# One core, a nine-stage network in fp32 split into two fp32r parts: named PSUM banks for each stage, a later place for one silu and for a stream of modulation columns, and the token sums of the sparse feed-forward layers all on VectorE

## The chip, the cores and the metric

The kernel runs on one core of one Trainium2 chip. The metric is the device time of one execution, in microseconds (us). TensorE is PE in the views, VectorE DVE, ScalarE ACT, GpSimd POOL, and SyncE, which here only issues DMAs, SP.

## The reference

The input is x (512 tokens x 1024 channels) and one conditioning vector c. Nine stages follow each other, each adding to x:

```python
cond = silu(c)
for l in (0, 1):
    sh1, sc1, g1, sh2, sc2, g2 = split(cond @ ada_w[l] + ada_b[l], 6)
    h = rmsnorm(x, norm_mix[l]) * (1 + sc1) + sh1
    y = even_mixer(h) if l == 0 else odd_mixer(h)      # attention: mix0, mix1
    x = x + g1 * (y @ w_out[l])
    h = rmsnorm(x, norm_ffn[l]) * (1 + sc2) + sh2
    x = x + g2 * ((silu(h @ gate[l]) * (h @ up[l])) @ down[l])   # ffn0, ffn1
x = x + mamba2(rmsnorm(x))      # ssm: chunked scan, 4 groups, 4 chunks of 128 tokens
x = x + swiglu(rmsnorm(x))      # ffn2
x = x + conformer(rmsnorm(x))   # conv
x = x + swiglu(rmsnorm(x))      # ffn3
out = rmsnorm(x)                # final
```

Mixer 0 has a differential attention and one over the 128 keys that an index score selects, mixer 1 a banded attention with sinks. All is fp32.

## The kernel before

x lies transposed in SBUF as eight tiles `xT` of 128 channels x 512 tokens. Every fp32 operand of a product is split into `hi` (a cast to fp32r, on ACT, L297 for weights) and `lo` (the rest, by a subtraction on DVE, L298 for weights), and each product is three matmuls, `hi` with `hi`, `lo` with `hi`, `hi` with `lo` (`mm3`, L305 to L307). Weights come in 512 KB pieces, `raw`, by DMAs that SP issues in one order; three `raw` and four `hi`/`lo` buffers circulate, so SP waits for a `lo` to be made before it can issue the next `raw`.

The stages run in the order mix0 (to about 350 us), ffn0 (367 to 740), mix1, ffn1 (947 to 1305), ssm (to 1715), ffn2 (1716 to 2080), conv, ffn3 (2302 to 2655), final. Between two stages the norm of the next one is spread over the last products of the one before: `sq` and its sum, PE's column sum `ss`, a chain of thirteen small DVE steps for the inverse root (L345 to L362), `rb`, four transposes by which PE spreads the result over partitions, then either `z` (L483) with `hi` and `lo` (L489 to L497, by ACT, POOL and DVE) in two column halves (class `Split`, before ffn0, mix1, ffn1, conv), or a copy `R` (L427) that multiplies the products afterwards (class `Norm`, before ssm, ffn2, ffn3).

In a feed-forward stage `gu([j])` computes gate `pg` and up `pu` of hidden block j, DVE and ACT make `s = silu(pg) * pu` and its split `d`, and `dn` multiplies five or so blocks by the down weights. Where `FIRST_S` says so (ffn1 from block 3, ffn2 and ffn3 from block 2), `gu7` replaces a gate/up pair by seven products of half the columns (`seven`): it needs sums of weight pieces (`ws`, L716 to L720) and sums of token pieces, which `crossed` makes once in a stage for four k: two subtractions (L693, L694), two more steps on DVE (L695, L696), a cast `xh` on ACT (L698) and the rest `xl` (L699). The subtractions are on POOL; `xl` is on DVE for even k and on POOL for odd k. `sums(ks)` is called within the items of the first blocks: in ffn1 all four k in the first item, in ffn2 and ffn3 two k in each of the first two.

In ffn0 a second stream runs beside the blocks: `md0.stream` and `md1.stream` make 56 columns of the modulation, for each a DMA `araw` (six buffers) and a reduction on DVE against `cb`, the broadcast silu of c (L657). `cond()` (L629) issues the DMA of `cb` and its Silu on ACT (L632). `behind` holds the stream back until the instruction `nm.mark`, the last `z` of the norm, has been placed, and `_weave` mixes the two streams by their weights, 345 and 28.

In ssm, `ssd(g)` handles a group in four chunks: products `pS`, `po`, `py` on PE, the sums `yo` and `yg` on DVE, the gated `zs` (L1507), its square on ACT (L1508), at the end of the group the thirteen small steps, the scaling of `zs` (L1523) and the transposes `yT`, which the last items `so(3)` need. The items `so(q)` (products `pj` of 512 columns) of earlier groups are woven in.

The program is written as such generators; the order in which an engine then executes its instructions is set when the kernel is built, by the scheduler of the Tile framework (`schedule_with_timeline_sim=True`), which goes by data, buffers and its own account of time. So an edit in one stage can change the order in others. PSUM has eight banks of 128 x 512 fp32; a stage's pool gives each tag (`mm`, `lg`, `tr`, `py`, `st`) a number of them that circulate:

```python
"ffn": ({"d": 12, "z": 6, "su": 2, "sq": 2, ...}, {"mm": 6, "st": 1, "tr": 1}),
...
return p.tile(shape, dt, tag=tag, name=name, bufs=bufs[tag])
```

Of the kernel before, what the change touches and what calls it, by code (L numbers as in the profile page):

```python
# [10 lines left out]
F32 = mybir.dt.float32  # L11
F32R = mybir.dt.float32r
I32 = mybir.dt.int32
AF = mybir.ActivationFunctionType
# [76 lines left out]
def _layout(i):  # L91
# [20 lines left out]
    for n in range(4):  # L112
# [36 lines left out]
PHASES = {  # L149
# [9 lines left out]
    "ssm": (SSB,  # L159
# [3 lines left out]
}  # L163
# [49 lines left out]
def chain(*gs):  # L213
    for g in gs:
        yield from g
# [7 lines left out]
def _program(nc, tc, a, out, stages=STAGES):  # L223
# [6 lines left out]
    sm = pool("sm", 4)  # L230
    cur = {"sb": None, "ps": None}

    def phase(name, kinds=("sb", "ps")):
        for k in kinds:
            if cur[k]:
                cur[k][0].close()
            e = ExitStack()
            kw = {"space": PSUM} if k == "ps" else {}
            p = e.enter_context(tc.tile_pool(name=f"{k}_{name}", bufs=1, reuse_waits="tile", **kw))
            cur[k] = (e, p, PHASES[name][k == "ps"])  # L240

    def ptile(k, shape, dt, name):
        tag = ALIAS.get(name, name)
        _, p, bufs = cur[k]
        if k == "ps" and tag not in bufs:
            tag = {"tr": "pt", "st": "tr", "py": "tr"}[tag]
        return p.tile(shape, dt, tag=tag, name=name, bufs=bufs[tag])

# [182 lines left out]
    class Split:  # L431
# [44 lines left out]
        def build(self, hf):  # L476
            o = HALVES[hf]
            for c in range(KC):
# [8 lines left out]
                if c % 2:  # L487
                    if sh is not None:
                        S.activation(z, z, AF.Identity, bias=sh)  # L489
                    S.copy(hi_, z)  # L490
                    self.gmark = G.tensor_tensor(lo, z, hi_.bitcast(F32), op=OP.subtract)
                elif sh is not None:
                    S.activation(hi_, z, AF.Identity, bias=sh)
                    V.scalar_tensor_tensor(lo, z, sh, hi_.bitcast(F32), op0=OP.add, op1=OP.subtract)  # L494
                else:
                    S.copy(hi_, z)
                    V.tensor_tensor(lo, z, hi_.bitcast(F32), op=OP.subtract)  # L497

# [130 lines left out]
    def cond():  # L629
        cbx[0] = wide("cb")  # L630
        nc.sync.dma_start(cbx[0], a["c"].to_broadcast([128, 1024]))
        S.activation(cbx[0], cbx[0], AF.Silu)  # L632

# [52 lines left out]

    def crossed(k, z1, z2, pool_lo):


        hv = T // 2  # L690
        t = wide1("ws")
        q = [t[:, i * hv:(i + 1) * hv] for i in range(4)]
        G.tensor_tensor(q[0], z1[:, :hv], z1[:, hv:], op=OP.subtract)  # L693
        G.tensor_tensor(q[2], z2[:, hv:], z1[:, hv:], op=OP.subtract)  # L694
        V.scalar_tensor_tensor(q[1], z2[:, hv:], -1.0, q[0], op0=OP.mult, op1=OP.subtract)  # L695
        V.scalar_tensor_tensor(q[3], q[1], -1.0, z2[:, :hv], op0=OP.mult, op1=OP.subtract)  # L696
        hi, lo = wide1("xh", F32R), wide1("xl", F32R)
        S.copy(hi, t)  # L698
        (G if pool_lo else V).tensor_tensor(lo, t, hi.bitcast(F32), op=OP.subtract)  # L699
        return [(hi[:, i * hv:(i + 1) * hv], lo[:, i * hv:(i + 1) * hv]) for i in range(4)]  # L700
# [49 lines left out]
    def ffn(n, nm, gcol, nxt):  # L750
# [6 lines left out]
        def sums(ks):  # L757
            for k in ks:
                z = []
                for c in (k, k + 4):  # L760
# [4 lines left out]
                    else:  # L765
                        z.append(tmp("z"))
                        S.activation(z[-1], X[c], AF.Copy, scale=nm.gcol(c))
                x4.append(crossed(k, *z, k % 2))
        d = {}

        def gu(js):
            def it():
# [14 lines left out]
                if sparse and len(x4) < 4:  # L787
                    sums(range(4) if direct else range(2 * js[0], 2 * js[0] + 2))
                if nm.R is None:
# [188 lines left out]
    def mix0(make, following):  # L978
        phase("mix0", ("sb",))
        phase("start", ("ps",))  # L980
        cond()
        consts()
# [817 lines left out]
    if stages[0] != "mix0":  # L1800
# [3 lines left out]
        if stages[0] in STAGES[:4]:  # L1804
            cond()
            mods()
            _run(chain(md0.stream(range(24)), md1.stream(range(24))))
        nm = norms[stages[0]]().all()
    for i, name in enumerate(stages):
# [14 lines left out]
        else:  # L1824
            n = int(name[3])
            f = ffn(n, nm, (None, md0.col(40), md1.col(40))[n + 1] if n < 2 else None, nx)
            if n == 0:
                cond()
                _weave((f, 345), (behind(lambda: nm.mark, chain(md0.stream(range(20, 24)), md1.stream(range(24)))), 28))
            else:  # L1830
                _run(f)
# [20 lines left out]
```

## Time and profile before

| | |
|---|---|
| three runs | 2678.31 us median (2671.75 to 2680.00) |
| profiled execution | 2678.19 us, of which the span in the trace is 2676.4 us |
| PE busy | 2526.0 us, 94% of the span |
| DVE, ACT, POOL busy | 1964.1 us (73%), 1264.7 us (47%), 529.5 us (20%) |
| mean granted TensorE clock | 0.977 of full speed |

The span begins with the first instruction and ends with the last; 1.8 us of the execution lie outside it. A line of a timeline gives the start from the span's beginning; in brackets stand the idle time of the engine just before and what released it, where that was a wait. The granted clock is 1.00 at 2.4 GHz and 0.5 at 1.2 GHz; a figure between is a mean over a stretch.

### The profile page before, as it was taken

What the parts mean: (1) busy time and instruction counts of PE and PEld (TensorE: products, weight loads), DVE (VectorE), ACT (ScalarE), POOL (GpSimd) and SP (SyncE); (2) the same over time, 40 slices, a digit from 0 to 9 for tenths busy, and PEclk for the clock granted to TensorE, in tenths of its full rate; (3) what the DMA queues carried; (4) which work ended last, traced back from release to release, by engine and by line L of the source; (5) the groups of instructions that cost most, each with busy time, mean ns of one, the idle gap of its engine ahead of it and who ended that gap; (6) DMA issues with size and microseconds to landing.
All of it is one profiled execution on the core that took longest, in us unless ns stands there. A gap on an engine that the chain in (4) does not pass through costs nothing.

```text
span 2676.4 us, 40109 instructions
## 1 busy us (share of the span) xinstructions
PE 2526.0 (94%) x15299; PEld 2230.7 (83%) x15299; DVE 1964.1 (73%) x3490; ACT 1264.7 (47%) x2353; POOL 529.5 (20%) x411
## 2 busy tenths in 40 slices
PE   5788989999999989999999999999999998899997
PEld 3666878888888989999788888789998888799997
DVE  7898765555556686677678886677877897677777
ACT  4456642222257554444455444444444555544443
POOL 3344220000022250000100000211101782311102
PEclk9988999999999999999999999999999998999999
DMA  7611125554521123333322121232333210233332
GB/s 269 230 56 40 32 87 204 173 173 163 176 82 40 40 64 95 110 93 103 106 75 73 51 83 60 79 92 86 108 98 115 72 63 17 71 103 103 103 103 80
DMA packets 89058, 265.81 MB, mean 99 GB/s; under 512 B 9760, under 2 KB 16032, under 8 KB 88864
## 3 DMA queue, kind: packets, MB, share of 16 engines
q1 hardware_dynamic: 88864, 263.24, 30.6%
q8 instruction: 120, 1.97, 0.3%
q14 instruction: 74, 0.61, 0.1%
HBM read 261.10 MB, written 2.10 MB: 98 GB/s over the span
## 4 chain that ended last, share of the span: by engine, by line
PE 55%; issue 17%; DVE 16%; DMA 4%; ACT 4%; POOL 3%; DVEq 0%; SPq 0%; POOLq 0%; ACTq 0%
PE pj L305 8%; PE pj L306 7%; PE pj L307 7%; PE pg L307 4%; PE pg L305 4%; PE pg L306 4%; DVE lo L298 4%; PE pu L307 3%; PE pu L306 3%; PE pu L305 3%; DMA raw<-w_gu 2%; DMA araw<-ada 1%; POOL yp L1615 1%; PE pj L1418 1%; PE pj L1419 1%
## 5 line engine op out<-in xcount | busy, mean ns | idle before, releaser
L297 ACT CAST hi<-raw 128x1024 fp32r<-128x1024 f32 (+5 forms) x454 | 395.1, 879 | 671.3 <-PE pj L306 236.6
L298 DVE TENSOR_TENSOR lo<-raw,hi 128x1024 fp32r<-128x1024 f32 (+4 forms) x444 | 465.7, 1052 | 181.8 <-ACT hi L297 179.4
L305 PE MATMUL pj<-d,hi 128*128 128x512 f32 (+1 forms) x968 | 354.4, 377 | 4.6 <-DVE s L822 1.6
L306 PE MATMUL pj<-d,hi 128*128 128x512 f32 (+1 forms) x968 | 357.2, 372 | 0.4 <-DVE d L390 0.4
L307 PE MATMUL pj<-d,lo 128*128 128x512 f32 (+1 forms) x968 | 353.6, 372 | 0.0
L747 POOL TENSOR_TENSOR bu<-bu 128x256 f32<-128x256 f32 x59 | 88.6, 1503 | 818.2 <-ACT bu L743 747.3
L305 PE MATMUL pu<-hi 128*128 128x256 f32 (+1 forms) x736 | 229.3, 313 | 2.3 <-DVE z L483 2.3
L307 PE MATMUL pu<-hi,lo 128*128 128x256 f32 (+1 forms) x736 | 230.4, 313 | 1.0 <-DVE lo L298 0.6
L306 PE MATMUL pu<-lo,hi 128*128 128x256 f32 (+1 forms) x736 | 228.8, 312 | 0.0
L305 PEld LDWEIGHTS pj<-d,hi 128*128 128x128 f32 x968 | 182.0, 190 | 37.8 <-DVE s L822 2.0
L305 PE MATMUL pj<-hi 128*128 128x512 f32 (+2 forms) x520 | 206.5, 400 | 4.4 <-ACT qk L907 1.2
L306 PEld LDWEIGHTS pj<-d,hi 128*128 128x128 f32 x968 | 183.8, 190 | 32.0 <-issue 1.0
L307 PEld LDWEIGHTS pj<-d,lo 128*128 128x128 f32 x968 | 183.4, 190 | 31.4 <-issue 0.5
L306 PE MATMUL pj<-lo,hi 128*128 128x512 f32 (+2 forms) x520 | 206.3, 397 | 3.3 <-DVE lo L494 1.4
L307 PE MATMUL pj<-hi,lo 128*128 128x512 f32 (+2 forms) x520 | 204.0, 393 | 0.3 <-DVE lo L298 0.3
L305 PE MATMUL pg<-xh,hi 128*128 128x256 f32 x708 | 199.7, 282 | 0.4 <-ACT ua L740 0.2
L307 PE MATMUL pg<-hi,lo 128*128 128x256 f32 (+1 forms) x572 | 191.9, 335 | 8.6 <-DVE lo L298 8.5
L307 PE MATMUL pg<-xh,lo 128*128 128x256 f32 x708 | 198.1, 280 | 0.0
L306 PE MATMUL pg<-xl,hi 128*128 128x256 f32 x708 | 198.1, 280 | 0.0
L305 PE MATMUL pg<-hi 128*128 128x256 f32 (+1 forms) x572 | 191.4, 335 | 6.7 <-DVE z L483 3.4
L306 PE MATMUL pg<-lo,hi 128*128 128x256 f32 (+1 forms) x572 | 191.0, 334 | 1.0 <-DVE lo L494 0.9
L297 ACT CAST hi<-ws 128x1024 fp32r<-128x1024 f32 x118 | 123.0, 1049 | 111.8 <-DVE ws L717 57.4
(485 smaller groups left out, 6419.7 us busy)
## 6 DMA issues: line engine op xcount, KB each, us to landing
raw<-w_gu SPq DMA_DIRECT2D x176, 512.0 KB, 3.8
araw<-ada SPq DMA_DIRECT2D x96, 512.0 KB, 6.0
raw<-w_dn SPq DMA_DIRECT2D x72, 320.0 KB, 2.9
raw<-w_p SPq DMA_DIRECT2D x24, 512.0 KB, 3.6
raw<-w_dn SPq DMA_DIRECT2D x24, 384.0 KB, 3.3
raw<-w_out SPq DMA_DIRECT2D x32, 256.0 KB, 2.8
raw<-w_xs SPq DMA_DIRECT2D x16, 512.0 KB, 3.5
raw<-w_z SPq DMA_DIRECT2D x16, 512.0 KB, 3.4
```

What stands on the lines that cost most here:

```text
L297: S.copy(hi, raw)
L298: (eng or V).tensor_tensor(lo, raw, hi.bitcast(F32), op=OP.subtract)
L305: E.matmul(ps, lh, rh, start=start, stop=False, **k)
L306: E.matmul(ps, lh, rl, start=False, stop=False, **k)
L307: E.matmul(ps, ll, rh, start=False, stop=stop, **k)
L747: G.tensor_tensor(bu[:, :hv], bu[:, :hv], bu[:, hv:], op=OP.add)
L1418: E.matmul(o, xh[:, ts], wh[:, k], start=st_, stop=False, skip_group_check=True)
L1419: E.matmul(o, xh[:, ts], wl[:, k], start=False, stop=False, skip_group_check=True)
L1615: G.tensor_tensor(yp[:, sft:], yp[:, sft:], pr[:, sft:], op=OP.add)
```

## The change

Each stage now names the banks of each tag as a tuple, the tags go round them in order (`turn`), and a stage's pool allocates all eight banks at its start. The number of banks of a tag does not change in any stage. `sq` gets three buffers in place of two in mix0, ffn0, ffn2 and ffn3, `d` ten in place of twelve in ffn2 and ffn3. In ffn0 the Silu of `cb` is issued by a small generator after four steps of the second stream, the stream waits for the last `lo` on DVE (`lmark`) and not for the last `z`, and its weight is 30. `crossed` makes all its subtractions and all `xl` on DVE. In ffn1 the token sums are made two k at a time, in the first two items.

```diff
 PHASES = {
-    "start": ({}, {"pi": 5, "pw": 1, "st": 1, "tr": 1}),
+    "start": ({}, {"pi": (0, 1, 2, 3, 4), "pw": (5,), "st": (6,), "tr": (7,)}),
-    "mix0": ({..., "yn": 3, "sq": 2, "re": 2, "rl": 2}, {"mm": 2, "lg": 3, "tr": 2, "py": 1}),
+    "mix0": ({..., "yn": 3, "sq": 3, "re": 2, "rl": 2}, {"mm": (0, 1), "lg": (2, 3, 4), "tr": (6, 7), "py": (5,)}),
-             {"mm": 2, "lg": 2, "tr": 2, "py": 1, "st": 1}),
+             {"mm": (5, 3), "lg": (0, 4), "tr": (1, 2), "py": (7,), "st": (6,)}),
-    "ffn0": ({"araw": 6, "cb": 2, "d": 16, "z": 3, "su": 2, "sq": 2}, {"mm": 6, "st": 1, "tr": 1}),
+    "ffn0": ({"araw": 6, "cb": 2, "d": 16, "z": 3, "su": 2, "sq": 3}, {"mm": (5, 3, 0, 4, 1, 2), "st": (6,), "tr": (7,)}),
+             {"mm": (7, 1, 5, 0, 3, 4), "st": (6,), "tr": (2,)}),
-    "ffn": ({"d": 12, "z": 6, "su": 2, "sq": 2, ...}, {"mm": 6, "st": 1, "tr": 1}),
+    "ffn": ({"d": 10, "z": 6, "su": 2, "sq": 3, ...}, {"mm": (2, 1, 5, 0, 3, 4), "st": (6,), "tr": (7,)}),
-            {"mm": 2, "lg": 2, "tr": 2, "py": 1, "st": 1}),
+            {"mm": (3, 4), "lg": (5, 0), "tr": (2, 1), "py": (7,), "st": (6,)}),
-             {"mm": 4, "pt": 2, "ac": 1, "st": 1}),
+             {"mm": (5, 0, 3, 4), "pt": (2, 1), "ac": (7,), "st": (6,)}),
...
+            if k == "ps":
+                turn.clear()
+                for b in range(8):
+                    p.tile([128, T], F32, tag=f"b{b}", name=f"b{b}", bufs=1)
...
+        if k == "ps":
+            i = turn[tag] = turn.get(tag, -1) + 1
+            return p.tile(shape, dt, tag=f"b{bufs[tag][i % len(bufs[tag])]}", name=name, bufs=1)
         return p.tile(shape, dt, tag=tag, name=name, bufs=bufs[tag])
...
-                    V.scalar_tensor_tensor(lo, z, sh, hi_.bitcast(F32), op0=OP.add, op1=OP.subtract)
+                    self.lmark = V.scalar_tensor_tensor(lo, z, sh, hi_.bitcast(F32), op0=OP.add, op1=OP.subtract)
...
     def cond():
...
-        S.activation(cbx[0], cbx[0], AF.Silu)
+        return lambda: S.activation(cbx[0], cbx[0], AF.Silu)
...
-    def crossed(k, z1, z2, pool_lo):
+    def crossed(z1, z2):
...
-        G.tensor_tensor(q[0], z1[:, :hv], z1[:, hv:], op=OP.subtract)
-        G.tensor_tensor(q[2], z2[:, hv:], z1[:, hv:], op=OP.subtract)
+        V.tensor_tensor(q[0], z1[:, :hv], z1[:, hv:], op=OP.subtract)
+        V.tensor_tensor(q[2], z2[:, hv:], z1[:, hv:], op=OP.subtract)
...
-        (G if pool_lo else V).tensor_tensor(lo, t, hi.bitcast(F32), op=OP.subtract)
+        V.tensor_tensor(lo, t, hi.bitcast(F32), op=OP.subtract)
...
                 if sparse and len(x4) < 4:
-                    sums(range(4) if direct else range(2 * js[0], 2 * js[0] + 2))
+                    sums(range(len(x4), len(x4) + 2))
...
             if n == 0:
-                cond()
-                _weave((f, 345), (behind(lambda: nm.mark, chain(md0.stream(range(20, 24)), md1.stream(range(24)))), 28))
+                silu = cond()
+
+                def later():
+                    for _ in range(4):
+                        yield 0.5
+                    silu()
+                    yield 0.0
+
+                _weave((f, 345), (chain(later(), behind(lambda: nm.lmark, chain(md0.stream(range(20, 24)),
+                                                                               md1.stream(range(24))))), 30))
```

Lines of the changed kernel stand ten higher from `lin` on (L494 is L504, L657 is L667). The order of the instructions changes at these places.

DVE at the start of ffn0, before: `lo<-z` is the norm's last split, `araw` a modulation reduction with its `mod` result, `lo<-raw` the split of a weight.

```order
L494 SCALAR_TENSOR_TENSOR lo<-z,mod_95,hi 128x256
L657 ISA araw,mod_95<-araw,cb,vec 128x1024
L657 ISA mod_95 128x1
L657 ISA araw,mod_95<-araw,cb,vec 128x1024
L657 ISA mod_95 128x1
L657 ISA araw,mod_95<-araw,cb,vec 128x1024
L657 ISA mod_95 128x1
L298 TENSOR_TENSOR lo<-raw,hi 128x1024
L797 TENSOR_TENSOR s<-s,pu 128x512
```

The same place after the change:

```order
L504 SCALAR_TENSOR_TENSOR lo<-z,mod_103,hi 128x256
L667 ISA araw,mod_103<-araw,cb,vec 128x1024
L667 ISA mod_103 128x1
L667 ISA araw,mod_103<-araw,cb,vec 128x1024
L667 ISA mod_103 128x1
L308 TENSOR_TENSOR lo<-raw,hi 128x1024
L807 TENSOR_TENSOR s<-s,pu 128x512
L308 TENSOR_TENSOR lo<-raw,hi 128x1024
L400 TENSOR_TENSOR d<-s,d 128x512
```

Before, three more `araw` reductions stood ahead of this L494, so six came ahead of the first weight's `lo`; now two do, and the next come after three weights. SP issues the loads in the same pattern.

PE at the end of ssm, before: the last `py` of the last group and what follows it (`pj` are products of the items `so`).

```order
L306 MATMUL pj<-d,hi 128x512
L307 MATMUL pj<-d,lo 128x512
L1503 MATMUL py<-xdt,L 128x64 x8
L305 MATMUL pj<-d,hi 128x512
L306 MATMUL pj<-d,hi 128x512
```

After the change, down to the transposes `yT`:

```order
L316 MATMUL pj<-d,hi 128x512
L317 MATMUL pj<-d,lo 128x512
L1504 MATMUL pS<-xd,bn 128x512
L1513 MATMUL py<-xdt,L 128x64 x8
L1498 MATMUL po<-Sst,xc 128x512
L1513 MATMUL py<-xdt,L 128x64 x8
L384 MATMUL yT<-cst,zs 128x128 x8
```

Before, 24 `pj` products stood between the last `py` and `yT`; now they stand ahead, and the products of the last two chunks follow each other directly.

PE at the start of ffn2, before: `rb` spreads the inverse root, `pg` and `pu` are gate and up of block 1 (512 columns), then of the first `gu7` (256 columns).

```order
L305 MATMUL pu<-hi 128x512
L306 MATMUL pu<-lo,hi 128x512
L374 MATMUL rb<-cst,rstd 128x128 x4
L307 MATMUL pu<-hi,lo 128x512
L305 MATMUL pg<-hi 128x512
```

After the change:

```order
L317 MATMUL pu<-hi,lo 128x512
L315 MATMUL pg<-hi 128x256
L316 MATMUL pg<-lo,hi 128x256
L384 MATMUL rb<-cst,rstd 128x128 x4
L317 MATMUL pg<-hi,lo 128x256
```

`rb` moved behind the rest of block 1, thirteen matmuls of 512 columns, and two of 256. In ffn3 it moved in the same way.

## Rows read from the trace of the kernel before

**Rows 1.** Page of the profiled execution, part 1: busy time of each engine, share of the span, instructions.
```profile
PE 2526.0 (94%) x15299; PEld 2230.7 (83%) x15299; DVE 1964.1 (73%) x3490; ACT 1264.7 (47%) x2353; POOL 529.5 (20%) x411
```

**Rows 2.** Timeline of PE, the matmuls at eight places that came after a wait: start (us from the span's start), duration, engine, line, operation, out<-in, matrix, shape, count, and in brackets the idle time before it and what ended that. In order of time: ffn0 (two), ffn1, ssm, ffn2 (two), ffn3 (two).
```profile
370.89 0.35 PE L305 MATMUL pg<-hi 128*128 128x256 f32 x1 [3.35 <-DVE z L483]
...
402.05 0.79 PE L307 MATMUL pg<-hi,lo 128*128 128x512 f32 x1 [4.92 <-DVE lo L298]
...
979.51 0.50 PE L307 MATMUL pg<-hi,lo 128*128 128x512 f32 x1 [1.77 <-DVE lo L298]
...
1688.01 1.62 PE L374 MATMUL yT<-cst,zs 128*128 128x128 f32 x8 [2.25 <-DVE zs L1523]
...
1716.53 0.47 PE L305 MATMUL pg<-hi 128*128 128x512 f32 x1 [0.56 <-DVE xT L685]
...
1746.39 0.38 PE L305 MATMUL pu<-xh,hi 128*128 128x256 f32 x1 [2.66 <-ACT hi L297]
...
2302.76 0.47 PE L305 MATMUL pg<-hi 128*128 128x512 f32 x1 [1.84 <-DVE xT L683]
...
2332.63 0.58 PE L305 MATMUL pu<-xh,hi 128*128 128x256 f32 x1 [2.66 <-ACT hi L297]
```

**Rows 3.** Timeline of ACT, 365 to 420 us (ffn0), columns as in rows 2.
```profile
382.80 1.06 ACT L632 ACTIVATE cb<-cb 128x1024 f32<-128x1024 f32 x1 [9.52 <-DMA cb<-c]
...
394.07 1.05 ACT L297 CAST hi<-raw 128x1024 fp32r<-128x1024 f32 x1 [4.93 <-PE pg L306]
...
405.78 1.05 ACT L297 CAST hi<-raw 128x1024 fp32r<-128x1024 f32 x1 [2.53 <-DMA raw<-w_gu]
```

**Rows 4.** Timeline of DVE, 380 to 420 us (ffn0).
```profile
389.62 1.76 DVE L657 CUSTOM_DVE_ANT_0 araw<-araw,cb,vec 128x1024 f32<-128x1024 f32 x1
...
393.66 1.28 DVE L657 CUSTOM_DVE_ANT_0 araw<-araw,cb,vec 128x1024 f32<-128x1024 f32 x1 [0.67 <-DMA araw<-ada]
...
396.88 1.29 DVE L657 CUSTOM_DVE_ANT_0 araw<-araw,cb,vec 128x1024 f32<-128x1024 f32 x1 [1.93 <-DMA araw<-ada]
...
399.57 1.28 DVE L657 CUSTOM_DVE_ANT_0 araw<-araw,cb,vec 128x1024 f32<-128x1024 f32 x1 [1.40 <-DMA araw<-ada]
...
400.78 1.22 DVE L298 TENSOR_TENSOR lo<-raw,hi 128x1024 fp32r<-128x1024 f32 x1
```

**Rows 5.** Busy times of each engine in two stretches of ffn0: stretch, its length, busy us of PE, of PE's weight loads, DVE, ACT and POOL (instructions), mean granted TensorE clock as a share of full speed, busy share of the DMA engines, GB/s.
```profile
397.10:402.10 5.00, 0.08 (x2) 0.05 (x1) 3.60 (x6) 0.89 (x2) 0.00 (x0) 0.78 0.04 15
402.10:409.00 6.90, 6.90 (x21) 5.52 (x22) 6.10 (x7) 2.19 (x3) 0.00 (x0) 0.66 0.79 254
```

**Rows 6.** Timeline of DVE, 964 to 982 us (ffn1).
```profile
967.95 0.95 DVE L695 SCALAR_TENSOR_TENSOR ws<-z,ws 128x256 f32<-128x256 f32 x1 [0.63 <-POOL ws L693]
...
973.23 4.56 DVE L699 TENSOR_TENSOR xl<-ws,xh 128x1024 fp32r<-128x1024 f32 x2
...
977.71 1.74 DVE L298 TENSOR_TENSOR lo<-raw,hi 128x1024 fp32r<-128x1024 f32 x1
...
979.98 0.41 DVE L695 SCALAR_TENSOR_TENSOR ws<-z,ws 128x256 f32<-128x256 f32 x1
980.31 1.21 DVE L298 TENSOR_TENSOR lo<-raw,hi 128x1024 fp32r<-128x1024 f32 x1
```

**Rows 7.** Busy times as in rows 5, ffn1.
```profile
980.00:985.00 5.00, 5.00 (x17) 3.93 (x16) 5.00 (x7) 2.31 (x4) 1.97 (x2) 0.66 0.67 205
```

**Rows 8.** Timeline of PE, 1733 to 1744 us (ffn2).
```profile
1737.29 0.60 PE L374 MATMUL rb<-cst,rstd 128*128 128x128 f32 x4
...
1740.70 0.28 PE L305 MATMUL pg<-hi 128*128 128x256 f32 x1
```

**Rows 9.** Timeline of DVE, 1736 to 1757 us (ffn2).
```profile
1738.54 0.69 DVE L800 TENSOR_TENSOR s<-pg,R 128x512 f32<-128x512 f32 x1 [3.11 <-ACT R L427]
...
1744.58 0.68 DVE L717 TENSOR_TENSOR ws<-ws,raw 128x512 f32<-128x512 f32 x1
...
1751.98 2.22 DVE L298 TENSOR_TENSOR lo<-ws,hi 128x1024 fp32r<-128x1024 f32 x1 [1.11 <-ACT hi L297]
```

**Rows 10.** Timeline of POOL, the same stretch.
```profile
1747.88 5.24 POOL L699 TENSOR_TENSOR xl<-ws,xh 128x1024 fp32r<-128x1024 f32 x1 [5.65 <-ACT xh L698]
```

**Rows 11.** Busy times as in rows 5, ffn2.
```profile
1749.10:1755.20 6.10, 5.81 (x26) 5.52 (x27) 4.99 (x6) 3.25 (x5) 4.02 (x1) 0.52 0.28 89
```

**Rows 12.** Timeline of PE, 1668 to 1692 us (end of ssm); a product that is not fp32r has two records, so x2 is one `po` and x16 one `py` of eight products.
```profile
1674.48 1.02 PE L1488 MATMUL po<-Sst,xc 128*128 128x512 f32 x2
...
1678.31 1.89 PE L1503 MATMUL py<-xdt,L 128*128 128x64 f32 x16
```

**Rows 13.** Timeline of DVE, the same stretch.
```profile
1680.24 0.69 DVE L1505 TENSOR_TENSOR yg<-yg,py 128x512 f32<-128x512 f32 x1 [0.44 <-PE py L1503]
...
1682.50 0.17 DVE L345 TENSOR_SCALAR rm<-gss 128x4 f32<-128x4 f32 x1 [0.79 <-ACT yg L1508]
...
1687.47 1.67 DVE L1523 TENSOR_SCALAR zs<-zs,gr 128x512 f32<-128x512 f32 x4
```

**Rows 14.** Busy times as in rows 5, mix0.
```profile
150.00:200.00 50.00, 41.25 (x196) 33.26 (x195) 50.00 (x143) 27.51 (x58) 28.78 (x18) 0.86 0.17 54
...
250.00:270.00 20.00, 11.64 (x55) 8.81 (x53) 15.19 (x36) 12.87 (x31) 11.53 (x9) 0.66 0.08 27
```

**Rows 15.** Timeline of the DMA queue of SP, 340 to 440 us: issue, time until the last of the count was issued.
```profile
402.02 0.33 SPq L291 DMA_DIRECT2D raw<-w_gu  x1
```

More of the change, by code (lines that the diff above doesn't have):

```diff
@@ L231, in _program @@
     cur = {"sb": None, "ps": None}
+    turn = {}
     def phase(name, kinds=("sb", "ps")):
@@ L493, in build @@
                     S.activation(hi_, z, AF.Identity, bias=sh)
-                    V.scalar_tensor_tensor(lo, z, sh, hi_.bitcast(F32), op0=OP.add, op1=OP.subtract)
+                    self.lmark = V.scalar_tensor_tensor(lo, z, sh, hi_.bitcast(F32), op0=OP.add, op1=OP.subtract)
                 else:
                     S.copy(hi_, z)
-                    V.tensor_tensor(lo, z, hi_.bitcast(F32), op=OP.subtract)
+                    self.lmark = V.tensor_tensor(lo, z, hi_.bitcast(F32), op=OP.subtract)
         def lin(self, sets, at=(5, 10)):
@@ L767, in sums @@
                         S.activation(z[-1], X[c], AF.Copy, scale=nm.gcol(c))
-                x4.append(crossed(k, *z, k % 2))
+                x4.append(crossed(*z))
         d = {}
@@ L980, in mix0 @@
         phase("start", ("ps",))
-        cond()
+        cond()()
         consts()
@@ L1804, in _program @@
         if stages[0] in STAGES[:4]:
-            cond()
+            cond()()
             mods()
@@ L1827, in _program @@
             if n == 0:
-                cond()
-                _weave((f, 345), (behind(lambda: nm.mark, chain(md0.stream(range(20, 24)), md1.stream(range(24)))), 28))
+                silu = cond()
[6 more added lines that the diff above has]
+                                                                               md1.stream(range(24))))), 30))
             else:
```

9 rows, old and new, of the table PHASES are left out of this document.

## The prediction, on record before the result

> **What bounds the kernel now.** I read the busy shares first, then PE's idle times with what ended each, then the timeline of the engine that ended it, last the granted clock of these stretches. PE is busy for 94% of the span [rows 1] and none of its matmuls is removed, so the change can only alter the 150 us in which PE waits and the time it spends at half clock. The reader should see that these waits stand where one stage hands over to the next: 4.92 us for a `lo` of DVE in ffn0, 1.77 us for one in ffn1, 2.25 us for `zs` at the end of ssm, 2.66 us for a `hi` in ffn2 and again in ffn3, and three on a bank [rows 2].
>
> **The change, part by part.**
>
> *Silu later.* `later()` counts steps of the second stream, but in ACT's order the Silu of `cb` keeps its place, and on SP `cb` still stands behind the seventh `w_gu`. ACT went idle 9.52 us for it [rows 3]; that stays: 0.
>
> *Modulation stream behind `lmark`.* Two things move, as the order shows. On DVE the last `lo` of the norm (L494) no longer stands behind three `araw` reductions, and between it and the first weight `lo` (L298) there are two reductions instead of three. On SP six `araw` loads in one run become two, then `w_gu`, then two. In the trace three reductions waited 0.67, 1.93 and 1.40 us for their transfers, and the weight `lo` that PE needed at 397.13 ran at 400.78 [rows 4], although ACT had cast its `hi` by 395.12 [rows 3]. The second reduction, like the first without a wait, ended at 391.38 [rows 4]; with L494, half a us, ahead of it that is 391.9. The `lo` then starts with the cast, at 395.1, and is there by 396.4, before PE asks. The 4.92 us go. PE then ran on at half clock: from 402.1 to 409.0 the mean was 0.66 [rows 5], 6.9 x 0.34 = 2.3 us of lost work that go too. Sum **-7.2**; at the worst 0, if another transfer takes the place of the wait.
>
> *Banks.* The ring inside a stage is what it was; only the bank that a new stage begins with changes. The 3.35 us in ffn0 ended with a bank, which is now free; but PE then waits that much longer for the second column half, whose `hi` ACT makes only behind the Silu at 382.80 [rows 2, 3]: 0. At the start of ffn2 (0.56) and of ffn3 (1.84) nothing else is late: **-2.4**. Bounds 0 and -5.7.
>
> *Sums on DVE in ffn1.* DVE was free at 967.32, waited for a subtraction of POOL, then made two `xl` in 4.56 us while POOL ran, and began the weight `lo` at 977.71 [rows 6]. Alone, a 128x256 step takes 0.41 us (about 0.34 to the next) and a 128x1024 one 1.21. The new order has fifteen such steps and three `xl` ahead of that `lo`: 967.3 + 5.1 + 3.6 = 976.0, and the `lo` is there at 977.2, half a us before PE asks at 977.74. The 1.77 us go, and 5.0 x 0.34 = 1.7 us of half clock behind them [rows 7]. Sum **-3.4**; worst 0.
> The Trainium skill speaks against this part: Perfetto Trace Analysis, Optimizing Scalar/DVE Operations, says that GpSimd and VectorE share a read port of SBUF, so that moving work between these two might not help. The trace agrees that they slow each other (2.28 us for an `xl` beside POOL, 1.21 for the same shape without). By that rule this term would be 0 and the whole sum -1.2.
>
> *Sums on DVE in ffn2 and ffn3.* Here the order turns against the change. The subtractions and both `xl` now stand in DVE's chain of `rstd`, and the transposes `rb` that end this chain go to PE later: before at 1737.29, now behind the second 256-wide matmul, the first of which began at 1740.70 [rows 8]: 3.3 us, taking off the 0.35 us of `rb` itself. `R`, then L800 (1738.54), then L717 (1744.58) hang on it [rows 9]. Between these two DVE spent 6.0 us, waits included; now four products (2.4), four subtractions and two steps (2.0), L716 (1.2) and two products (1.2) stand there, 6.8 us. ACT's cast of `ws` and PE follow, so that PE resumes some 3.5 to 4 us later than 1746.39. What comes back: POOL's `xl` of 5.24 us [rows 10] becomes 1.2 on DVE, the `lo` of 2.22 us beside it [rows 9] also 1.2, and the spell at half clock, 0.52 from 1749.1 to 1755.2 [rows 11], has less work in it. I take the last product of that item 2.4 us later in ffn2 and, its wait being alike [rows 2], 2.7 in ffn3: **+5.1**. Bounds for each -1.3 (no delay, only the quicker `xl` and `lo`) and +4.
>
> *End of ssm.* No line of ssm is touched, but its order is. Before, PE's last `py` (1.89 us, ended 1680.20 [rows 12]) had 24 products of 0.227 us behind it, and `yT` came at 1688.01: 7.8 us, 5.5 of them covered. Now these products stand ahead, and `pS`, `py`, `po`, `py`, `yT` come in a row. PE was through with all of them at 1685.76; less 1.0 + 1.9 + 1.0 + 1.9 for those four [rows 12] it is 1679.9. From there: `pS` and the first `py` 2.9; DVE reads `py`, 0.7, which frees the one `py` bank for the next; then `zs`, `L`, `yo`, `yg`, beside which PE makes the last `py`, then `yg` + `py` and `zs`, six steps at about 0.67, 4.0; ACT's square, 0.75; thirteen small steps, which took 4.97 us with four 128x512 steps of about 0.6 among them and so take 2.5 alone; the first scaling, 0.5 [rows 13]. 1679.9 + 11.4 = 1691.3 against 1688.01: **+3.3**. Bounds +3.1 (from `py` to `yT` alone: 7.8 less the 2.4 of the interleaved steps, less the 2.25 waited before) and +5.6 (with 2.3 of half clock, as in ffn0).
>
> *mix0 and mix1.* The same instructions in another order. PE idled 8.75 us from 150 to 200, where DVE was busy for all 50.00 us, and 8.4 of the 20 us from 250 [rows 14]. The products that fill such places are spent earlier now, while fewer `py` break the first place. I take 0, and a third of these 17 us, 6, as bound on either side.
>
> *Buffers.* No wait on `sq` or `d` stands in the rows read, and a part of the hidden blocks needs ten `d`: 0.
>
> Sum: -7.2 - 2.4 - 3.4 + 5.1 + 3.3 = **-4.6 us**, made against the profiled execution's own 2678.2 us, which lies 0.1 us under the median of the runs: 2673.6 us. That is 0.2%; 0.3%, 8 us, is about what a measurement of this kernel can tell from no change.
>
> **Rivals.**
> A. *The hand-overs of ffn2 and ffn3 win too.* For it: the last releaser there may be the `lo` or POOL's `xl`, both of which get quicker, and not `rb`. Against it: `rb` is in front of every step up to L717. With -1.3 each in place of +5.1: -4.6 - 5.1 - 2.6 = -12.3, 2665.9 us.
> The Trainium skill's GPSIMD Engine Reference, Engine selection, would have it so: elementwise work belongs on VectorE, GpSimd being about twice as slow with two inputs. The trace agrees on POOL's step being the slower; that this decides the time is not in it.
>
> B. *In ffn0 the wait moves instead of going.* The eighth `w_gu` was issued at 402.02 [rows 15], when its buffer came free with the late `lo`, and ACT stood 2.53 us for it until 405.78 [rows 3]. That buffer comes free some 5.5 us earlier now, but PE asks 7.2 us earlier, each later `w_gu` shares SP's queue with pairs of `araw`, and a late `araw` holds the `lo` behind it on DVE. It decides if a transfer lands over 2 us later than this leaves. Then the 7.2 are not won, and three waits as long as those of before (0.67, 1.93 and 1.40 [rows 4]) with 2.3 of half clock come on top: -4.6 + 7.2 + 6.3 = +8.9, 2687.1 us.
>
> C. *The split does not do what it says:* naming banks frees nothing at ffn2 and ffn3 (+2.4): -2.2, 2676.0 us, inside the forecast's case.
>
> **How the numbers follow.** Forecast 0.37 and C 0.06, both no change that can be told: 0.43. A, or mix0 at its better bound: 0.38, faster. B, or ssm, ffn2, ffn3 and mix0 at their worse bounds: 0.19, slower. The range goes from A with most of mix0's bound, 2665.9 - 4.9 = 2661, to just over B, 2689.
>
> **What would show it.** In the profile after: no wait of PE over 1 us and clock 1.00 between 390 and 415; none on `lo` near 970; one of 5 to 6 us on `yT` at the end of ssm, in place of 2.25; the wait on `hi` of `ws` in ffn2 and ffn3 about 6 us in place of 2.66; no `ws` and `xl` on POOL. It is wrong if `yT` waits less than 4 us, if ffn2 and ffn3 resume no later after `rb`, or if PE's idle time in mix0 differs by over 6 us.

## The result, and the profile after

The changed kernel takes 2708.03 us (median of four runs, 2704.18 to 2711.90) against 2679.15 for the kernel before beside it: ratio 1.0113, 95% interval 1.0087 to 1.0139. Measured again (e9) it is 1.0130 (1.0111 to 1.0148). It is 30 to 35 us slower, where -4.6 was forecast; the range ended at 2689. The profiled execution has a span of 2703.7 us at a mean granted clock of 0.974.

The page of the changed kernel, part 1, beside [rows 1]:

```profile
PE 2537.0 (94%) x15299; PEld 2235.5 (83%) x15299; DVE 1971.6 (73%) x3520; ACT 1262.8 (47%) x2353; POOL 485.0 (18%) x381
```

PE has the same 15299 records of matmuls and is busy 11 us longer; the rest of the 27 us of span is idle time. The timeline of PE after the change, the matmuls behind its waits (columns as in [rows 2]), by stage: ffn0, ffn1, start of ssm, end of ssm, ffn2, conv, ffn3.

```profile
385.74 0.58 PE L316 MATMUL pg<-lo,hi 128*128 128x256 f32 x1 [2.87 <-DVE lo L504]
...
957.46 0.40 PE L316 MATMUL pg<-lo,hi 128*128 128x256 f32 x1 [2.79 <-DVE lo L504]
...
1370.32 0.63 PE L1460 MATMUL px<-cst,xc 128*128 128x128 f32 x4 [0.64 <-DVE yg L1465]
1371.52 0.63 PE L1460 MATMUL px<-cst,xc 128*128 128x128 f32 x4 [0.57 <-DVE yg L1465]
1373.16 1.13 PE L1504 MATMUL pS<-xd,bn 128*128 128x512 f32 x2 [1.01 <-DVE xd L1489]
...
1691.04 2.00 PE L1513 MATMUL py<-xdt,L 128*128 128x64 f32 x16 [1.12 <-DVE Sst L1509]
1693.82 1.13 PE L1498 MATMUL po<-Sst,xc 128*128 128x512 f32 x2 [0.78 <-DVE yg L1515]
1695.90 1.97 PE L1513 MATMUL py<-xdt,L 128*128 128x64 f32 x16 [0.96 <-DVE yo L1500]
1703.10 1.97 PE L384 MATMUL yT<-cst,zs 128*128 128x128 f32 x8 [5.23 <-DVE zs L1533]
...
1764.15 0.58 PE L315 MATMUL pu<-xh,hi 128*128 128x256 f32 x1 [6.06 <-ACT hi L307]
...
1766.08 0.58 PE L317 MATMUL pu<-xh,lo 128*128 128x256 f32 x1 [0.71 <-DVE lo L308]
...
1772.10 0.39 PE L315 MATMUL pg<-hi 128*128 128x256 f32 x1 [1.61 <-ACT hi L307]
...
2230.88 1.87 PE L1579 MATMUL st<-ones,cv 128*128 128x1 f32 x8 [5.37 <-DVE cv L1677]
...
2357.78 0.58 PE L315 MATMUL pu<-xh,hi 128*128 128x256 f32 x1 [6.06 <-ACT hi L307]
```

Read it against [rows 2]: the 4.92 near 400 and the 1.77 near 978 are gone, no wait on a bank is left at the starts of ffn2 and ffn3, and the 3.35 at the start of ffn0 has become 2.87. New are four waits before and at `yT` (8.1 us in place of 2.25), three at the start of ssm (2.2 together), 6.06 in place of 2.66 twice, and 5.37 in conv, where waits of 1.87 and 2.88 went. How long each stage lasts says more than single waits. The stages are cut at the same matmuls of PE in every trace (numbers 230, 1500, 3200, 4600, 6900, 9400, 11700, 12960 and 15220). These cuts do not lie right at the hand-overs: ssm's stretch holds the last 16 us of ffn1 and the first 9 of ffn2. The lengths in the profiled executions of this study, in us (their number in brackets; left out are those that change the stage or its neighbour in some other way):

| stage | stage as before | part of the change in it |
|---|---|---|
| mix0 | 263.0 to 265.9 (12 executions) | banks named: 267.2 to 268.9 (4); and three `sq`: 270.5 to 271.7 (3) |
| ffn0 | 364.7 to 370.1 (8; before 370.1) | stream later: 361.1 to 364.9 (10) |
| ssm | 439.1 to 441.9 (8) | banks named: 451.7 to 455.6 (7) |
| ffn2 | 338.4 to 343.3 (7) | all sums on DVE: 345.5 to 349.1 (7) |
| conv | 248.3 to 251.2 (11) | banks named: 250.2 to 255.0 (7) |
| ffn3 | 333.4 to 334.8 (12) | all sums on DVE: 337.0 to 342.0 (7) |

mix1 shows no difference (212 to 219 against 213 to 222). So a stage of the same order differs by 1 to 7 us from one execution to the next, and mix0, ssm, ffn2 and ffn3 lie wholly outside their own spread.

### The profile page after: what moved, and what is told of

Same layout as the page of the kernel before. It is cut to its first block, busy times and chain, and to the rows that moved or that the text cites. A ratio compares the mean times of both kernels' runs of the same rounds, so it can differ in the third digit from the quotient of the medians.

```text
span 2703.7 us, 40048 instructions
## 1 busy us (share of the span) xinstructions
PE 2537.0 (94%) x15299; PEld 2235.5 (83%) x15299; DVE 1971.6 (73%) x3520; ACT 1262.8 (47%) x2353; POOL 485.0 (18%) x381
```

## The experiments

Changes in us are the ratio against the kernel before, less one, times 2675.

**The parts apart.** e1 has the named banks of the change alone, e2 the token sums (`crossed` and `sums`), e3 the Silu and the stream of ffn0, e4 everything but the named banks.

```diff
 e1: all stages as in the change, buffer counts old; e4: the change without this
-            {"mm": 2, "lg": 2, "tr": 2, "py": 1, "st": 1}),
+            {"mm": (3, 4), "lg": (5, 0), "tr": (2, 1), "py": (7,), "st": (6,)}),
 e2
-        G.tensor_tensor(q[0], z1[:, :hv], z1[:, hv:], op=OP.subtract)
+        V.tensor_tensor(q[0], z1[:, :hv], z1[:, hv:], op=OP.subtract)
...
-        (G if pool_lo else V).tensor_tensor(lo, t, hi.bitcast(F32), op=OP.subtract)
+        V.tensor_tensor(lo, t, hi.bitcast(F32), op=OP.subtract)
...
-                    sums(range(4) if direct else range(2 * js[0], 2 * js[0] + 2))
+                    sums(range(len(x4), len(x4) + 2))
 e3
-                _weave((f, 345), (behind(lambda: nm.mark, chain(...)), 28))
+                _weave((f, 345), (chain(later(), behind(lambda: nm.lmark, chain(...))), 30))
```

> Named banks alone, everything else as in the kernel before. Theory T (naming the banks makes the scheduler place the instructions of mix0, ssm and conv in another order, and that order is what costs; the trace of the changed kernel lost 7.3 us in mix0, 13.4 in ssm, of which 5.5 at its end, and some 4 in start and conv): slower than before by 18 to 24 us, about 2700. Rival R1 (the reordering is neutral, as the prediction had it, except for 3.3 us at the end of ssm; the loss comes from the other parts that run beside it): +1 us, 2680. Rival R2 (the loss in mix0 and ssm is half each): +10, 2689.

Measured: 1.0065 (1.0044 to 1.0086), +17 us.

> The token sums alone: all on VectorE, and in ffn1 two k at a time; banks, stream, Silu and buffers as before. Theory T: ffn2 and ffn3 each lose 5 to 6 us (the changed kernel's wait on the cast of ws is 6.06 us in place of 2.66), ffn1 gains 3: +8 us, 2687. Rival (prediction's sizes): +1.7, 2681. Rival (POOL's share of the sums was what held PE back): -6, 2673.

Measured: 1.0022 (1.0010 to 1.0035), +6; beside the one profile of the kernel before, ffn2 is 3.7 and ffn3 3.2 us longer, ffn1 2.4 shorter.

> The later Silu and the stream of modulation columns behind lmark with weight 30 alone; all else as before. Theory T: the 4.92 us wait of ffn0 and the half clock behind it go: -7 us, 2672. Rival (the wait comes back at a later transfer): 0, 2679.

Measured: 0.9990 (0.9981 to 1.0000), -3. The wait is gone, as expected; the gain is less than half.

> The whole change without the named banks: sums on VectorE, stream and Silu, buffer counts. Theory T: the sum of the parts, +8 - 7 + 0 for the buffers: +1 us, 2680, so all but 1 to 5 us of the 28 us by which the changed kernel is slower goes. Rival (the parts do not add, the buffers or sums reorder mix0 and ssm as the banks do): over +10, 2690 or more.

Measured: 1.0016 (1.0002 to 1.0030), +4. The loss is in naming the banks first, in the sums of ffn2 and ffn3 second. Why e3 gains 3 and not 7 can be read in the other profiles: the ten executions of this study with the old stream have at this place waits of 4.92 (the kernel before), 3.42, 2.23, 3.44, 3.16, 1.71, 0.96, 3.80, 1.61 and 2.48 us, a mean of 2.8; the ten with the new one have none over 0.3. The wait that the forecast was read from is the longest of its ten.

**What naming does.** The builder's tile numbers give the order in which the program asks for tiles. In the kernel before, each of the 1034 PSUM tiles is first written by PE behind all lower-numbered tiles of its tag. In the changed kernel some 30 tiles go ahead of a lower-numbered one: nine in mix0, six in mix1, twelve in ssm, and a few in conv and at the ends of the feed-forward stages. mix0, mix1, ssm and conv are the stages in which most of PE's rows moved without an edit. The first case in ssm, in PE's order before and with ssm's banks named (row, line, tiles):

```
before  6274 L374  MATMUL bt_12657<-cst_73,xc_12535 128x128 x4
        6275 L1335 MATMUL bt_12664<-cst_73,vt_12613 128x32 x4
named   6247 L1344 MATMUL bt_12672<-cst_73,vt_12621 128x32 x4
        6273 L383  MATMUL bt_12665<-cst_73,xc_12543 128x128 x4
```

A tag with a count is one queue for its banks, and its banks do not come in turn: the builder gave `tr` of ssm the banks 3, 4, 3, 3, 4 first and `mm` 0, 1, 1, 0, likely the one that it counts as free first. A tag with named banks keeps a strict turn and is a queue for each bank, so a tile may pass one that waits for another bank. In the case above the two `bt` tiles had banks 4 and 3 before; named, the lower-numbered one has 3 and the one that passes it has 4. No run separates the strict turn from the passing; naming brings both. Three kernels name one tag of ssm each, e13 all five. In e6 and e13 every tag of ssm keeps the banks that it had; in e5 and e7 the two named ones are placed first, as banks 0 and 1, and the banks of some other tags move up.

```diff
 e13; alone: e6 mm (0, 1), e7 lg (5, 6), e5 tr (3, 4)
-            {"mm": 2, "lg": 2, "tr": 2, "py": 1, "st": 1}),
+            {"mm": (1, 0), "lg": (5, 6), "tr": (4, 3), "py": (7,), "st": (2,)}),
```

> Named banks for one tag of one stage: tr of ssm, two banks; all else as before. In the order three px or bt tiles now go ahead of an earlier tile of their tag, the start of ssm stays as it was, and at its end py, po, py, yT stand in a row with no pj between, as in the changed kernel. Theory T (a tag whose banks are named lets a later tile overtake an earlier one, and the overtaking sets the order that costs): yT waits 5.2 us in place of 2.25, py and po three waits of 0.8 to 1.1, the end of ssm loses 5.5 us, its start nothing: +5.5 us, 0.2%. Rival (the end costs what it does only together with the other reordering or with the bank numbers): 0.

Measured: 1.0030 (1.0017 to 1.0043), +8.

> Named banks for mm of ssm alone. One pj tile overtakes at the start of ssm; behind it 34 products pj stand ahead of px, pl and pS, which then follow without products between, and at the end of ssm 12 products lie between the last py and yT, half of the 24 before. Theory T: three waits of 0.6 to 1.0 us on px and pS at the start, +3 us there, and about +2 at the end, where half of the cover is left: +5 us, 0.2%. Rival (start and end both hidden): 0.

Measured: 1.0030 (1.0018 to 1.0042), +8. One wait of 1.03 at the start, not three; `yT` waits 3.62, and ffn2 waits 3.97 for its first bank in place of 0.56, which was not expected: by the strict turn the last sum of ssm now lies in bank 0, with which ffn2 begins, and before it lay in bank 1.

> Named banks for lg of ssm alone: seven tiles overtake, but neither the start nor the end of ssm changes its order (24 products stay between the last py and yT; the first pS keeps its place). Theory T (not the naming as such costs, but where PE is left without products): 0, yT waits 2.25 us as before. Rival (the named ring costs by itself, by its allocation of whole banks or its waits): +5 us or more.

Measured: 1.0001 (0.9990 to 1.0011), 0. Seven overtakings cost nothing.

> Named banks for all tags of ssm, with the numbers that its pool gave them before; the other stages as before. The order in ssm is that of the changed kernel. Theory T (the reordering costs, not the numbers): +12 us, waits on px and pS at the start and 5.2 us on yT at the end. Rival (most of the 12 came from other banks at the hand-overs): +5 or less.

Measured: 1.0050 (1.0034 to 1.0067), +13. ssm lasts 452.9 us, and its waits are those of the changed kernel to 0.01 us. PE's timeline at the end of ssm, `yT` in e5, e6 and e7, then three places of e13:

```profile
1695.84 1.97 PE L383 MATMUL yT<-cst,zs 128*128 128x128 f32 x8 [5.22 <-DVE zs L1532]
```
```profile
1689.38 1.97 PE L383 MATMUL yT<-cst,zs 128*128 128x128 f32 x8 [3.62 <-DVE zs L1532]
```
```profile
1680.95 1.63 PE L383 MATMUL yT<-cst,zs 128*128 128x128 f32 x8 [2.25 <-DVE zs L1532]
```
```profile
1367.99 1.12 PE L1503 MATMUL pS<-xd,bn 128*128 128x512 f32 x2 [1.01 <-DVE xd L1488]
...
1685.88 2.00 PE L1512 MATMUL py<-xdt,L 128*128 128x64 f32 x16 [1.12 <-DVE Sst L1508]
...
1697.94 1.97 PE L383 MATMUL yT<-cst,zs 128*128 128x128 f32 x8 [5.23 <-DVE zs L1532]
```

With 0, 12 and 24 products between the last `py` and `yT` the wait is 5.22, 3.62 and 2.25. At this place neither the naming (e7) nor other banks (e13 keeps them) cost, but an order in which PE has nothing left to put in. Cut at matmuls 9200 and 9300, round `yT`, e13 and then the kernel before:

```profile
1680.99:1711.92 30.93, 21.96 (x101) 16.60 (x100) 19.72 (x42) 10.66 (x23) 0.88 (x1) 0.83 0.08 25
```
```profile
1676.47:1701.66 25.19, 21.96 (x101) 17.14 (x100) 16.33 (x38) 8.64 (x15) 0.56 (x1) 0.93 0.15 49
```

PE is busy for the same 21.96 us in both, so the 5.7 us between them are idle time. The mean granted clock falls with it, from 0.93 to 0.83, and in these two executions that cost nothing of its own. In e9, e14, e17 and e18, with the same order here, it is 0.70 to 0.79 and the stretch takes 32.2 to 34.3 us.

**All stages but ssm.** e10 names every other stage as the change does.

```diff
-            {"mm": (3, 4), "lg": (5, 0), "tr": (2, 1), "py": (7,), "st": (6,)}),
+            {"mm": 2, "lg": 2, "tr": 2, "py": 1, "st": 1}),
```

> Named banks in every stage but ssm; all else as before. Tiles overtake in mix0 (8), mix1 (6) and conv (2); their order is that of the changed kernel. Theory T (most of the cost is in ssm, 13 us in two profiles; mix0 +3, mix1 -3, conv +2 to +4.6, starts of ffn2 and ffn3 -2.4): 0 to +4 us. Rival (mix0 is as bad as the profile of the changed kernel shows it, +7, and conv +4.6): +9.

Measured: 1.0047 (1.0033 to 1.0061), +13. This does not say what it was made for: ssm lasts 450.6 us, though nothing in it moved, because a stage with counted banks now meets one with named banks: as built, the last sum of ffn1 and the first product of ssm both have bank 0. PE waits 5.46 us at the start of ssm and 3.27 at that of ffn2, where the bank is 1. mix0, 268.9, is still some 4 above its usual length.

**Sums.** e8 moves only the `xl` of odd k to VectorE, e16 only the two subtractions.

```diff
 e8
-        (G if pool_lo else V).tensor_tensor(lo, t, hi.bitcast(F32), op=OP.subtract)
+        V.tensor_tensor(lo, t, hi.bitcast(F32), op=OP.subtract)
 e16
-        G.tensor_tensor(q[0], z1[:, :hv], z1[:, hv:], op=OP.subtract)
-        G.tensor_tensor(q[2], z2[:, hv:], z1[:, hv:], op=OP.subtract)
+        V.tensor_tensor(q[0], z1[:, :hv], z1[:, hv:], op=OP.subtract)
+        V.tensor_tensor(q[2], z2[:, hv:], z1[:, hv:], op=OP.subtract)
```

> Only the rest xl of odd k moves from POOL to VectorE; the subtractions stay on POOL, and all else as before. In the order the four rb of ffn2 stay where they were (with the subtractions on VectorE they come ten to fifteen products later). Theory T (the subtractions in VectorE's chain of rstd are what costs in ffn2 and ffn3, by the later rb; xl on VectorE is a gain): the wait on the cast of ws stays 2.66 us or less, ffn2 and ffn3 about -1 us each, ffn1 0 to -2: -2 to -4 us, 2671. Rival (any of the work moved to VectorE costs there): the wait grows to 4 us or more, +3 to +7.

Measured: 0.9991 (0.9980 to 1.0003), -2.

> Only the two subtractions of the token sums move from POOL to VectorE, in all three stages; xl stays split between POOL and VectorE, and ffn1 still makes all four k in the first item. In the order rb of ffn2 then stands ten products later. Theory T (these subtractions in the chain of rstd delay rb, and R, the sums of weight pieces and the cast of ws behind it): the wait on the cast of ws grows from 2.65 to 5 us or more, ffn2 and ffn3 lose 3 each, ffn1 0: +6 us. Rival (xl and subtractions cost only together): 0 to +2.

Measured: 1.0045 (1.0031 to 1.0059), +12, more than the +6 of e2, which moves `xl` too; ffn2 and ffn3 are 6 and 5 us above their usual length. Why it costs more than e2 is not explained. PE in ffn2, `rb` and the product that waits for the cast of `ws`, in e8 and in e16:

```profile
1735.01 0.60 PE L374 MATMUL rb<-cst,rstd 128*128 128x128 f32 x4
...
1744.11 0.39 PE L305 MATMUL pu<-xh,hi 128*128 128x256 f32 x1 [2.65 <-ACT hi L297]
...
1746.84 0.58 PE L307 MATMUL pu<-xh,lo 128*128 128x256 f32 x1 [2.00 <-DVE lo L298]
```
```profile
1737.09 0.60 PE L374 MATMUL rb<-cst,rstd 128*128 128x128 f32 x4
...
1746.38 0.58 PE L305 MATMUL pu<-xh,hi 128*128 128x256 f32 x1 [5.13 <-ACT hi L297]
...
1748.31 0.58 PE L307 MATMUL pu<-xh,lo 128*128 128x256 f32 x1 [0.71 <-DVE lo L298]
```

So the subtractions cost, and for `xl` no cost shows (its interval ends at +1). The DVE in ffn2 shows where: the last `rstd` of the kernel before, then of the changed kernel the last `rstd`, `s` and L727, the sum of weight pieces that the cast of `ws` waits for.

```profile
1733.75 0.15 DVE L362 SCALAR_TENSOR_TENSOR rstd<-rt,rstd 128x4 f32<-128x4 f32 x1
```
```profile
1750.11 0.16 DVE L372 SCALAR_TENSOR_TENSOR rstd<-rt,rstd 128x4 f32<-128x4 f32 x1
1756.11 0.69 DVE L810 TENSOR_TENSOR s<-pg,R 128x512 f32<-128x512 f32 x1 [5.85 <-ACT R L437]
...
1762.32 0.70 DVE L727 TENSOR_TENSOR ws<-ws,raw 128x512 f32<-128x512 f32 x1
```

And PE of the changed kernel in the same stretch:

```profile
1754.86 0.60 PE L384 MATMUL rb<-cst,rstd 128*128 128x128 f32 x4
```

`rstd` is there at 1750.27, and PE makes `rb` 4.6 us later; DVE stands idle 5.85 us for its result. In the kernel before `rstd` was there at 1733.90 and `rb` came at 1737.29 [rows 8], also 3.4 us later. In both, the place in PE's order decides when `rb` is made. It now stands fifteen matmuls further down, some 3.2 us; in its old place, at about 1751.7 by that estimate, it would have found `rstd` there. That the builder moved `rb` because it counts with a later `rstd` is likely, but not shown. So the delay is in PE's order, more than in DVE's work.

**Whole and parts.** e9 is the changed kernel again. e14 gives it the old buffer counts, e17 only mix0's two `sq`, e18 only those of ffn0, ffn2 and ffn3.

```diff
 e17 (e14: both)
-    "mix0": ({..., "yn": 3, "sq": 3, "re": 2, "rl": 2}, ...
+    "mix0": ({..., "yn": 3, "sq": 2, "re": 2, "rl": 2}, ...
 e18 (and "sq": 2 in ffn0)
-    "ffn": ({"d": 10, "z": 6, "su": 2, "sq": 3, ...
+    "ffn": ({"d": 12, "z": 6, "su": 2, "sq": 2, ...
```

> The changed kernel once more, beside the next three on one chip. Theory T (parts add): +17.5 for the named banks and +4.3 for the rest, measured apart, make +22 us against the kernel before. Rival (the parts make each other worse): +28 or more, 1.0105 as a ratio.

Measured: 1.0130 (1.0111 to 1.0148), +35; the parts, +17 (e1) and +4 (e4), add to 22.

> The changed kernel with the buffer counts of before (sq 2, d 12). 109 of PE's rows in mix0 then stand as in the kernel with named banks alone. Theory T (three sq let mix0 go into an order that costs some 4 us more once the banks are named): +26 us, 4 to 8 less than the changed kernel. Rival (the buffers are without effect, the parts are just larger together): +30 to +34.

Measured: 1.0076 (1.0061 to 1.0090), +20.

> The changed kernel with two sq in mix0 in place of three. Theory T (the third sq lets mix0 go into a worse order): +20 to +24 us, as with all the old counts. Rival (ffn2 and conv with ten d): +30 to +34, as the changed kernel.

Measured: 1.0088 (1.0071 to 1.0105), +24.

> The changed kernel with the old counts in ffn0, ffn2 and ffn3 (sq 2, d 12) and three sq in mix0. Theory T (mix0): +30 to +34 us. Rival (d and sq of the feed-forward stages, or conv's order behind them): +20 to +24.

Measured: 1.0105 (1.0091 to 1.0119), +28. With the old counts the parts do add (20 against 17 + 6 - 3). The buffers cost some 14 on top of named banks and about 1 without. The third `sq` accounts for 3 to 4 of them in mix0 (271.4 us in e18, 267.5 in e17); where the rest is the intervals of e17 and e18 do not settle.

**The parts that pay.** e11 keeps the stream of e3, `xl` on VectorE, and subtractions on VectorE, two k at a time, in ffn1 alone. e12 adds named banks in the feed-forward stages. e15 is e11 in which ffn2 and ffn3 take `st` and `tr` first, which moves the bank that `mm` begins with and no instruction.

```diff
 e11
-                x4.append(crossed(k, *z, k % 2))
+                x4.append(crossed(*z, V if direct else G))   # engine of the two subtractions
 e12, on top
-    "ffn0": (..., {"mm": 6, "st": 1, "tr": 1}),
+    "ffn0": (..., {"mm": (5, 3, 0, 4, 1, 2), "st": (6,), "tr": (7,)}),
...
 e15, on top of e11
         phase(("ffn1" if direct else "ffn") if sparse else "ffn0")
+        for t in ("ss", "rb") if n > 1 else ():
+            psum(t)
```

> The parts that pay, without named banks: the stream and the Silu of ffn0 as in the change; xl on VectorE everywhere; the subtractions on VectorE in ffn1 alone, two k at a time there; in ffn2 and ffn3 the subtractions stay on POOL. Theory T: -3 (stream, measured alone) - 2 (ffn1) - 1 to -2 (xl): -6 to -7 us, 2668. Rival (the gains cover the same time): -3.

Measured: 2666.14 us, 0.9965 (0.9952 to 0.9979), -9. It beats both kernels.

> The kernel before last with named banks in ffn0, ffn1 and ffn2/ffn3 alone, where no tile overtakes at a place where PE waits. Theory T: the waits on a bank at the start of ffn2 (0.56) and ffn3 (1.84) go, nothing else changes: 2 to 3 us faster than that one, -9 us. Rival (the named ring costs in itself): slower than that one by 3 or more.

Measured (the kernel that it names is e11): 1.0002 (0.9992 to 1.0011), 0, or some 10 worse than e11. Neither theory had the reason. PE at the starts of ssm and ffn2 in e12:

```profile
1302.55 0.76 PE L316 MATMUL pj<-hi 128*128 128x512 f32 x1 [5.87 <-DVE xT L692]
...
1719.14 0.47 PE L316 MATMUL pu<-hi 128*128 128x512 f32 x1 [3.27 <-DVE xT L696]
```

In ssm no row moved. As in e10, its first product gets the bank, 0, that ffn1's last sum is still being read from, and a product of ffn2's first block the bank, 1, of ssm's last sum. The bank at a stage's start is worth up to 6 us here.

> The kernel of the parts that pay, in which ffn2 and ffn3 take up st and tr first, so that mm begins with a bank that the stage before has long left; no bank is named and the order is the same. Theory T: the waits of 0.55 and 1.84 us at the starts of ffn2 and ffn3 go: 2 to 3 us faster than without, -10.5 us against the kernel before, 2664. Rival (PE waits for the next thing instead): -8, as without.

Measured: 2664.14 us, 0.9963 (0.9949 to 0.9977), -10. PE at the starts of ffn2 and ffn3 in e11, then in e15:

```profile
1708.66 0.47 PE L305 MATMUL pg<-hi 128*128 128x512 f32 x1 [0.54 <-DVE xT L685]
...
2291.38 0.47 PE L305 MATMUL pg<-hi 128*128 128x512 f32 x1 [1.84 <-DVE xT L683]
```
```profile
1712.97 0.40 PE L305 MATMUL pg<-hi 128*128 128x512 f32 x1
...
2293.47 0.39 PE L305 MATMUL pg<-hi 128*128 128x512 f32 x1
```

Both waits are gone. That the kernel is faster by them the two intervals cannot tell.

## Why the prediction was wrong

- *Banks* ("The ring inside a stage is what it was; only the bank that a new stage begins with changes"): **this step failed.** The ring did not stay what it was: the banks of a counted tag did not come in turn, those of a named one do, and some 30 tiles pass a lower-numbered one where none of 1034 did. The order in mix0, ssm and conv moved with it, and the whole part costs +17 (e1) in place of -2.4. The -2.4 for the starts was right in its waits, so rival C is out.
- *mix0 and mix1* ("The same instructions in another order", taken at 0, bound 6): the same error. Moved rows were seen, and their loss and gain were taken to cancel without a price for either. mix0 lost some 3.5 with the banks and 3 more with the third `sq`, a little beyond the bound; mix1 nothing. The sign named for it, PE's idle time, shows 36.4 us before and 38.6 after: of the 7.3 us in these two profiles, 5.1 are busy time. Why is not settled.
- *End of ssm* (+3.3): right place and mechanism, too small. Of the sum's steps the wait on `yT` came as told (5 to 6 forecast, 5.23 measured), but the three waits ahead of it, 2.86 together, were not in it. Between matmuls 9200 and 9300 the changed kernel takes 30.7 us against 25.2, +5.5, the prediction's worse bound, but by idle time and not by the half clock that this bound had in it. e5, which in ssm brings this end without the waits at the start, costs 8.
- *Start of ssm*: no term. Three waits of 2.2 us together. Between matmuls 7200 and 7500 the changed kernel takes 47.8 us against 44.3, +3.5, at a clock of 1.00 in both; that is most of the difference between e5 (+8) and e13 (+13).
- *conv*: no term, though its order moved as well; about 3 by the stage lengths, ranges overlapping.
- *Sums in ffn2 and ffn3* (+5.1): sign, chain and wait right (about 6 forecast, 6.06 measured). The size was half: these stages are longer by some 5 each in place of 2.6. Of the gains that the sum took off (3.5 to 4 became 2.4) the wait for `lo` did shrink, from 2.00 in e8 to 0.71, but the next gate product now waits 1.61 for a cast, so the whole delay stays. Rival A is out: the wait grew, and by e8 and e16 the later `rb` costs, while a quicker `xl` gains 2 us, no change within the interval. The Trainium skill's GPSIMD Engine Reference, Engine selection, would have put all of it on VectorE; the runs bear that out for `xl` at most (-2, no change within the interval), not for the subtractions (+12).
- *Sums in ffn1* (-3.4): right sign; 1.77 went, and a wait of 2.79 in place of 2.27 stands at the stage's start; ffn1 is some 1.6 shorter. By the rule of the Trainium skill's Perfetto Trace Analysis, Optimizing Scalar/DVE Operations, it would have been 0; the stage's gain lies between rule and forecast.
- *Stream of ffn0* (-7.2): mechanism right. Of the stretch behind the old wait, the clock is 1.00 where it was 0.66 [rows 5]:

```profile
398.00:415.00 17.00, 17.00 (x118) 15.86 (x117) 10.58 (x14) 6.88 (x10) 1.64 (x2) 1.00 0.45 152
```

  The size was read from one execution, the worst of ten: -3 (e3). Rival B did not occur.
- *Buffers* (0): right without named banks (about 1), wrong with them (some 14).

With the measured sizes by stage (mix0 +6.5, ffn0 -3, ffn1 -1.6, ssm +12.5, ffn2 +5, conv +3, ffn3 +5.5) the sum is +28, against 30 and 35 measured; the other few us are not placed. The signs that the prediction named for the profile all came (no wait over 1 us between 390 and 415, none near 970, 5.23 on `yT`, 6.06 twice, no `ws` and `xl` on POOL), except that the clock from 390 to 415 is 0.98; they test its terms, and the miss lies where it had no term or one of 0.

## What to carry to other kernels

When a scheduler fixes the order, ask of an edit which waits it no longer has to respect: here named banks turned one queue for each tag into one for each bank, some 30 tiles passed another, and the order that came of it cost 17 us, most of it in ssm. Passing by itself need not cost (seven in e7 cost nothing). A stage whose rows move gets a term and a range even if none of its lines is touched: look where PE has products left to put between a chain's last steps, and count them. And before a wait of one profile is booked as gain, ask whether transfers set it: the same place can wait 1 us in the next execution.

## What the runs showed that was not expected

- The wait behind the modulation stream in ffn0, which has DMA transfers in its chain, varies from 0.96 to 4.92 us at the same order of instructions, while the one on `yT`, between engines alone, is 2.24 or 2.25 us in eleven executions.
- The granted clock differs too between executions at the same order: from 1300 to 1310 us in ssm the kernel e4 has 0.66, where the kernel before has 1.00 from 1300 to 1320. Between matmuls 6972 and 7040, at the start of ssm, that is 16.9 us before and 17.9 to 19.7 in e2, e3, e4, e11 and e15, at a mean clock of 0.83 to 0.91.
- The input of `rb` was there for 4.6 us in ffn2, and for 3.4 in the kernel before, while PE made the products that stand ahead of it in the built order.
